# The first feed-forward product of a two-layer encoder by Strassen's algorithm in Winograd's form, over pairs of weight units

## The chip, the cores and the metric

One core of a Trainium2 chip runs the whole program. The metric is device time in microseconds (us) for one execution. The engines are TensorE (PE, matrix products; PEld is its weight load), VectorE (DVE), ScalarE (ACT), GpSimd (POOL) and SyncE (SP, here a DMA queue).

## The reference

Two post-norm layers over 512 tokens of 1024 features. Each layer has a token mixer (differential attention in layer 0, dilated window attention in layer 1), cross-attention into 256 memory tokens, and a gated feed-forward part with a centred depthwise convolution of width 3:

```python
def conv_glu(x, w_in, conv_w, conv_b, w_out):
    gate, val = jnp.split(x @ w_in, 2, axis=-1)
    gate = lax.conv_general_dilated(gate, conv_w[:, None, :], ...) + conv_b
    return (jax.nn.gelu(gate, approximate=False) * val) @ w_out
...
x = layer_norm(ALPHA * x + conv_glu(x, ...), ln_g[i, 2], ln_b[i, 2])
```

`w_in` is 1024 x 5632 (2816 gate columns and 2816 value columns) and `w_out` is 2816 x 1024. All data are float32.

## The kernel before

**Products.** Each float32 operand is split into a high part, rounded to the multiplier's format, and the low rest. `evac(src, hi, lo)` does it: ACT casts (L220), DVE subtracts (L221). `mm3` then adds three products in one PSUM bank (L241 high by high, L242 high by low, L243 low by high).

**Weights.** All weights lie in one array in the order of use. `fetch` brings the next unit of 128 x 1024 into one of four `raw` buffers through SP's queue, `split` makes its halves in one of six `whi` and `wlo` buffers, `unit()` hands out the oldest and keeps four more coming (`pump`).

**The feed-forward part.** `ffn` goes over 22 column blocks j of 128. Block j needs one unit of gate columns and one of value columns. `t_proj` multiplies a unit with all 512 tokens: 8 steps over the features, 3 products each, all 512 columns wide, into one bank. The activations `act` (`x1h`, `x1l` in layer 0) hold the 1024 features as 8 tiles of 128 by 512 tokens. `tail` then makes the hidden block: ACT scales the gate (L934), DVE adds the two neighbours (L936, twice), ACT applies gelu (L937), DVE multiplies with the value (L939), ACT and DVE split the result (L941, L942). Blocks 0 and 1 are multiplied in two halves of 256 tokens by `Halves`, the first half while the normalization before it still turns the last tokens. The hidden blocks' halves are then the stationary side of the second product (`OutNorm.finish`).

**Order.** The program on PE stands as it is written. On the other engines a scheduler sets the order from priorities; each engine then runs its list strictly in that order, and semaphores hold an instruction until its inputs are there and its output's buffer is free.

Of the kernel before, what the change touches and what calls it, by code (L numbers as in the profile page):

```python
# [20 lines left out]
NJ = FF // 128  # L21
# [128 lines left out]
def encoder(ctx: ExitStack, tc: tile.TileContext, wall, xin, lam, subln, conv, lngb, tabf, tabd, eye, out):  # L150
# [19 lines left out]
        nc.tensor.matmul(ps, warm[:, :128], warm, start=True, stop=True)  # L170


    state = {"off": 0, "n": 0}
# [43 lines left out]
    def evac(ps, hi, lo, scale=None):  # L217

        if scale is None:
            nc.scalar.copy(hi, ps)  # L220
            nc.vector.tensor_tensor(lo, ps, hi.bitcast(F32), op=ALU.subtract)  # L221
# [15 lines left out]
        while due:  # L237
            due.pop(0)[1]()

    def mm3(ps, ah, al, bh, bl, start, stop):  # L240
        nc.tensor.matmul(ps, ah, bh, start=start, stop=False)  # L241
        nc.tensor.matmul(ps, ah, bl, start=False, stop=False)  # L242
        nc.tensor.matmul(ps, al, bh, start=False, stop=stop)  # L243
        n = 1
        for d in ps.shape[1:]:
            n *= d
        tick(max(3 * 216 * n // 512, 324))

    def bank(pool, tag):
        return pool.tile([128, 512], F32, tag=tag, name="ps_" + tag)  # L250

    def sl(k, n=128):
        return slice(k * n, k * n + n)

    def t_proj(ps, act, n=SEQ):

        xh, xl = act
        wh, wl = unit()
        for k in range(8):
            mm3(ps[:, :n], wh[:, sl(k)], wl[:, sl(k)], xh[:, k, :n], xl[:, k, :n], k == 0, k == 7)  # L260
            yield 3 * 216 * n // 512

    class Halves:


        def __init__(self, pss, act):
            self.pss, self.act = pss, act
            self.us = [unit() for _ in pss]
            self.half(0)
# [8 lines left out]
    def run(gen):  # L278
        for _ in gen:
            pass  # L280
# [26 lines left out]
        for fill in fills[cur:]:  # L307
            run(fill[0])

    def new_act(name):  # L310
        h = acts.tile([128, 8, 512], F32R, tag="ah", name=name + "h")
        l = acts.tile([128, 8, 512], F32R, tag="al", name=name + "l")
        return h, l

    def places(where):

# [11 lines left out]
    class OutNorm:  # L328

        def __init__(self, ln, nk, ktile):
            self.ln, self.nk, self.ktile = ln, nk, ktile
# [104 lines left out]
        def turn(self, q, n, xs, act, ps):  # L438
            tps = ps.rearrange("p (a b) -> p a b", b=128)
            for k in range(4):  # L440
                nc.tensor.transpose(tps[:, k, :], xs[:, sl(n * 4 + k)], ident)
            pe["now"] += 440
            d = (slice(None), sl(n, 4), sl(q))
            with tc.high_priority(offset=URGENT):
                evac(tps, act[0][d], act[1][d])


    def mem_load(mt):
# [474 lines left out]
        run(late)  # L923


    def ffn(l, act, pz, hs, led):
        with ExitStack() as c:
            gp = c.enter_context(tc.tile_pool(name=f"gp{l}", bufs=2, reuse_waits="tile"))
            cw = gp.tile([128, NJ, 4], F32, name="cw", bufs=1)
            nc.scalar.dma_start(cw, conv[l])  # L930

            def tail(j, pg, pv):
                g = gp.tile([128, 512], F32, tag="g", name="g")
                nc.scalar.activation(g, pg, AF.Identity, bias=cw[:, j, 3:4], scale=cw[:, j, 1:2])  # L934
                for w, d, n in ((2, g[:, 0:511], pg[:, 1:512]), (0, g[:, 1:512], pg[:, 0:511])):
                    nc.vector.scalar_tensor_tensor(d, n, cw[:, j, w:w + 1], d, op0=ALU.mult, op1=ALU.add)  # L936
                nc.scalar.activation(g, g, AF.Gelu)  # L937
                h = gp.tile([128, 512], F32, tag="h", name="h")
                nc.vector.tensor_tensor(h, g, pv, op=ALU.mult)  # L939
                hi, lo = hs(j)  # L940
                nc.scalar.copy(hi, h)  # L941
                nc.vector.tensor_tensor(lo, h, hi.bitcast(F32), op=ALU.subtract)  # L942

            led.half(1)
            pss = led.pss
            tail(0, pss[0], pss[1])
            tail(1, pss[2], pss[3])
# [9 lines left out]

    act = new_act("x")
    res = xin
    mems = [{}, {}]  # L960
    U = [1024] * 8
    for l in range(2):
        if l == 0:
            expect(*U, *U, *([1024] * 4))
        else:
            for p in range(LH // 2):
                expect(*([1024] * (6 if p % 2 else 12)))
        expect(*U, lambda m=mems[l]: mem_load(m.get("mt")))
        expect(*U, *U, *U, *U, *([1024] * (3 * NJ)))
    for l in range(2):  # L970
        mt_kv = mems[l]
        oT = new_act(f"o{l}")
# [2 lines left out]
        with ExitStack() as cz:  # L975
# [40 lines left out]
                mem_values(mt_kv["mt"], kv, pz)  # L1016
            oT = new_act(f"c{l}")
            o2 = oT
            on = OutNorm(3 * l + 1, 8, lambda k, o_=o2: (o_[0][:, k, :], o_[1][:, k, :]))
# [3 lines left out]
            act, res, led = on.finish(lambda q: [bank(pz, "t" if q == 2 else "o") for _ in range(2)],  # L1023
                                      [(((0, 0), (1, 0)), (2, 3))], res, False,
                                      lambda q: (pa, "a") if q == 0 else (pz, "s"),
                                      lambda a: Halves([bank(pa, "a"), bank(pz, "o"), bank(pa, "a"), bank(pz, "o")], a))
            c2.close()
            with ExitStack() as c:
                fp = c.enter_context(tc.tile_pool(name=f"ff{l}", bufs=1, reuse_waits="tile"))
                f8 = new_act(f"f{l}")  # L1030
                g8 = [fp.tile([128, 2, 512], F32R, tag=f"g{n}", name="g") for n in range(NJ - 8)]

                def hs(j, f8=f8, g8=g8):
                    return tuple(x[:, j, :] for x in f8) if j < 8 else (g8[j - 8][:, 0, :], g8[j - 8][:, 1, :])

                ffn(l, act, pz, hs, led)
# [3 lines left out]
                act, res, led = OutNorm(3 * l + 2, NJ, hs).finish(  # L1040
                    lambda q: [bank(*where[q]) for _ in range(2)], first, res, l == 1,
                    lambda q: where[q] if q < 2 else (pz, "s"),
                    lambda a: Halves([bank(pa, "a"), bank(pa, "a"), bank(pz, "t"), bank(pz, "t")], a) if a else None,
                    lambda n, dt=F32: fp.tile([128, D], dt, tag=f"g{n}", name="row"))
            if l == 0:
                cpz = cz.pop_all()

# [33 lines left out]
```

## Time and profile before

| | |
|---|---|
| three runs, median | 1879.43 us (1879.33 to 1879.47) |
| the profiled execution | 1878.97 us, its span 1877.1 us |
| PE busy | 1859.6 us, 99% of the span |
| DVE, ACT, POOL busy | 51%, 40%, 6% of the span |
| granted TensorE clock | 0.999 |

A row of grouped instructions has the line, engine, operation, the tile written and the tiles read, shapes, the count, total busy us and mean ns of one; what follows the second bar is the engine's idle time ahead of them and what ended it. A row of the timeline has its start and length in us; x counts merged instructions.

### The profile page before, as it was taken

The page shows a single profiled execution, that of the slowest core. Times are in us where ns is not written, and L with a number is a line of the kernel's source. Part 1 is how long each engine was busy: PE and PEld are TensorE (multiplying, and loading weights), DVE is VectorE, ACT ScalarE, POOL GpSimd, SP SyncE. Part 2 cuts the span into 40 slices and gives each one's busy share as a digit, 9 for nine tenths or more (in the row PEclk, how much of TensorE's full clock was granted, in tenths as well). Part 3 has the DMA queues.
Part 4 walks back from the last instruction along what each step waited for, and adds up shares of the span by engine and source line. Part 5 has one row for each costly group of instructions (what it writes and reads, how often), then busy time and mean ns, then how long its engine had stood idle before and what let it go on. Part 6 is the DMA issues. An engine that isn't in the chain of part 4 may idle for free.

```text
span 1877.1 us, 25119 instructions
## 1 busy us (share of the span) xinstructions
PE 1859.6 (99%) x9896; PEld 1582.4 (84%) x9896; DVE 950.0 (51%) x1761; ACT 751.9 (40%) x1356; POOL 116.6 (6%) x192
## 2 busy tenths in 40 slices
PE   9999999999999999999999999999999999999998
PEld 7888888889888888898898898987888898888886
DVE  5687684556444432533444444444855564444324
ACT  4476554424333322324434344344544343333211
POOL 0011120010000000100000000002200100000000
PEclk9999999999999999999999999999999999999999
DMA  7233175134232334333223222232752253323241
GB/s 247 72 92 89 35 251 173 60 123 156 93 101 93 98 101 145 104 130 102 79 82 95 83 85 85 80 91 57 245 182 79 104 156 101 93 98 101 90 146 45
DMA packets 60293, 208.55 MB, mean 111 GB/s; under 512 B 8336, under 2 KB 8976, under 8 KB 60176
## 3 DMA queue, kind: packets, MB, share of 16 engines
q1 hardware_dynamic: 48512, 172.19, 29.1%
q0 software_dynamic: 10944, 33.76, 5.4%
q8 instruction: 78, 1.28, 0.3%
q10 hardware_dynamic: 720, 1.01, 0.2%
q14 instruction: 39, 0.32, 0.1%
HBM read 190.01 MB, written 12.71 MB: 108 GB/s over the span
## 4 chain that ended last, share of the span: by engine, by line
PE 90%; DVE 5%; issue 2%; ACT 1%; DMA 1%; POOL 1%; POOLq 0%; DVEq 0%; ACTq 0%
PE ps_a L241 17%; PE ps_a L242 16%; PE ps_a L243 16%; PE ps_o L241 7%; PE ps_o L243 7%; PE ps_o L242 7%; PE ps_s L243 2%; PE ps_s L242 2%; PE ps_s L241 2%; PE ps_t L243 2%; PE ps_t L241 2%; PE ps_t L242 2%; PE S L714 1%; PE ps_t L801 1%; PE ps_t L782 1%
## 5 line engine op out<-in xcount | busy, mean ns | idle before, releaser
L221 DVE TENSOR_TENSOR wlo<-raw,whi 128x1024 fp32r<-128x1024 f32 (+1 forms) x309 | 376.8, 1220 | 468.2 <-ACT whi L220 463.3
L220 ACT CAST whi<-raw 128x1024 fp32r<-128x1024 f32 (+1 forms) x309 | 323.2, 1048 | 588.7 <-PE ps_a L242 258.3
L241 PE MATMUL ps_a<-x2h,whi 128*128 128x512 f32 (+1 forms) x384 | 149.3, 389 | 0.0
L243 PE MATMUL ps_a<-x2h,wlo 128*128 128x512 f32 (+1 forms) x384 | 146.5, 381 | 0.0
L242 PE MATMUL ps_a<-x2l,whi 128*128 128x512 f32 (+1 forms) x384 | 146.3, 381 | 0.0
L241 PE MATMUL ps_a<-whi,x2h 128*128 128x512 f32 (+1 forms) x256 | 88.8, 347 | 0.0
L242 PE MATMUL ps_a<-wlo,x2h 128*128 128x512 f32 (+1 forms) x256 | 87.2, 341 | 0.0
L243 PE MATMUL ps_a<-whi,x2l 128*128 128x512 f32 (+1 forms) x256 | 87.2, 341 | 0.0
L243 PEld LDWEIGHTS ps_a<-x2h,wlo 128*128 128x128 f32 x384 | 72.2, 188 | 14.1
L241 PEld LDWEIGHTS ps_a<-x2h,whi 128*128 128x128 f32 x384 | 72.3, 188 | 13.9
L242 PEld LDWEIGHTS ps_a<-x2l,whi 128*128 128x128 f32 x384 | 72.3, 188 | 12.8
L728 ACT ACTIVATE u<-u,st 128x256 f32<-128x256 f32 x128 | 63.6, 499 | 22.8 <-DVE st L726 22.7
L241 PE MATMUL ps_o<-x1h,whi 128*128 128x512 f32 (+1 forms) x192 | 71.6, 373 | 0.0
L241 PE MATMUL ps_o<-x4h,whi 128*128 128x512 f32 (+1 forms) x192 | 71.6, 373 | 0.0
L242 PE MATMUL ps_a<-x1l,whi 128*128 128x512 f32 (+1 forms) x192 | 71.3, 371 | 0.0
L242 PE MATMUL ps_a<-x4l,whi 128*128 128x512 f32 (+1 forms) x192 | 71.3, 371 | 0.0
L241 PE MATMUL ps_a<-x1h,whi 128*128 128x512 f32 (+1 forms) x192 | 71.3, 371 | 0.0
L241 PE MATMUL ps_a<-x4h,whi 128*128 128x512 f32 (+1 forms) x192 | 71.3, 371 | 0.0
L243 PE MATMUL ps_a<-x1h,wlo 128*128 128x512 f32 (+1 forms) x192 | 71.3, 371 | 0.0
L243 PE MATMUL ps_a<-x4h,wlo 128*128 128x512 f32 (+1 forms) x192 | 71.3, 371 | 0.0
L243 PE MATMUL ps_o<-x1h,wlo 128*128 128x512 f32 (+1 forms) x192 | 71.3, 371 | 0.0
L243 PE MATMUL ps_o<-x4h,wlo 128*128 128x512 f32 (+1 forms) x192 | 71.3, 371 | 0.0
(422 smaller groups left out, 4483.7 us busy)
## 6 DMA issues: line engine op xcount, KB each, us to landing
raw<-in_wall_dram SPq DMA_DIRECT2D x314, 512.0 KB, 3.5
y<-row POOLq DMA_DIRECT2D x40, 256.0 KB, 2.8
row<-y POOLq DMA_DIRECT2D x20, 512.0 KB, 5.6
row<-in_lngb_dram POOLq DMA_DIRECT2D x12, 512.0 KB, 4.9
k<-k SPq DMA_DIRECT2D x16, 256.0 KB, 2.9
F<-fd POOLq DMA_DIRECT2D x16, 256.0 KB, 5.0
row<-in_x_dram POOLq DMA_DIRECT2D x4, 512.0 KB, 8.6
out_dram<-row SPq DMA_DIRECT2D x8, 256.0 KB, 2.0
```

The source lines that it names most:

```text
L220: nc.scalar.copy(hi, ps)
L221: nc.vector.tensor_tensor(lo, ps, hi.bitcast(F32), op=ALU.subtract)
L241: nc.tensor.matmul(ps, ah, bh, start=start, stop=False)
L242: nc.tensor.matmul(ps, ah, bl, start=False, stop=False)
L243: nc.tensor.matmul(ps, al, bh, start=False, stop=stop)
L714: nc.tensor.matmul(Ss[b, c][:, f], q_[h, b, :], k_[h], start=True, stop=True)
L728: nc.scalar.activation(u[:, f], u[:, f], AF.Exp, bias=m, scale=-1.0, accum_out=s[:, b, 2 * c + 1:2 * c + 2])
L782: nc.tensor.transpose(tp[:, k, :], u[:, sl(k)], ident)
L801: nc.tensor.matmul(o[sl(c, 64), sl(2 * (n // 2) + x)], V[:, :64], PTs[2 * x + c][:, n, :], start=n % 2 == 0, stop=n % 2 == 1)
```

## The change

Blocks 2 to 20 of each layer, 19 pairs of a gate unit and a value unit, are no longer multiplied by `t_proj`. A pair is a 2 by 2 block matrix: gate and value, each with its first four feature tiles (`a`) and its last four (`b`). The activations are 2 by 2 as well: features 0 to 511 and 512 to 1023, tokens 0 to 255 (`h0`) and 256 to 511 (`h1`). Winograd's form of Strassen's algorithm forms this product with seven half products of 4 feature tiles by 256 tokens in place of eight.

* `pair` fetches both units, forms four sums of weights on POOL (s1 to s4, L957, in the order s1, s2, s4, s3) and splits three of the four halves and the four sums, in pieces of 512 columns: seven `evac`. The sums live in two buffers. Up to two pairs are kept ahead.
* The four sums of activations (T1 to T4) are formed on POOL once per layer (L1002), from copies `xr` of the activations that ACT makes in `OutNorm.turn` (L447).
* `early`, `seventh`, `middle` and `last` are the products and the additions that join them, on ACT (L1025, L1034, L1035) and DVE (L1026, L1041, L1047). Round m multiplies early(m), seventh(m-1), middle(m), last(m-1), so that a pair's end lies in the round after its start. Each pair has two banks, and a third product may add to a bank only after the sum before it is read.
* `mix` replaces `tail`, with the gate now read from the SBUF tile `G`. The split of the hidden blocks moves to `part`, after the pairs: blocks 0 to 7 before the last block's gate product is through, 8 to 19 after its value product, 20 and 21 at the very end. Block 21 is multiplied as before.

The diff, cut:

```diff
-    def ffn(l, act, pz, hs, led):
...
-            for j in range(2, NJ):
-                pg, pv = bank(pa, "a"), bank(pz, "o")
-                run(t_proj(pg, act))
-                run(t_proj(pv, act))
-                tail(j, pg, pv)
+    def ffn(l, act, pz, H, f8, led, raw, store, pairs, ready):
...
+        def sums():
+            return [sw.tile([128, 512], F32R, tag=t, name=t, bufs=n) for t, n in (("sh", 5), ("sl", 6))]
+        def pair():
+            if len(pairs) > 1:
+                return False
+            g, v = fetch(1024), fetch(1024)
+            a, b = slice(0, 512), slice(512, 1024)
+            with tc.high_priority(offset=LATER):
+                gh, gl = halves()
+                vh, vl = halves()
+                for s in (b, a):
+                    evac(g[:, s], gh[:, s], gl[:, s])
+                S = [sums() for n in range(4)]
+                s1, s2, s4, s3 = (gp.tile([128, 512], F32, tag="s", name="s") for n in range(4))
+                for n, (o, p, q, op) in enumerate(((s1, v[:, a], v[:, b], ALU.add), (s2, s1, g[:, a], ALU.subtract),
+                                                   (s4, g[:, b], s2, ALU.subtract),
+                                                   (s3, g[:, a], v[:, a], ALU.subtract))):
+                    nc.gpsimd.tensor_tensor(o, p, q, op=op)
+                for n, o in enumerate((s1, s2, s3, s4)):
+                    evac(o, *S[n])
+                    if n == 1:
+                        evac(v[:, b], vh[:, a], vl[:, a])
...
+        def product(ps, a, b, more=False):
+            for k in range(4):
+                t = sl(k)
+                mm3(ps, a[0][:, t], a[1][:, t], b[0][:, k, :], b[1][:, k, :], k == 0 and not more, k == 3, more)
...
+        def mix(j, pg, pv):
+            g = gp.tile([128, 512], F32, tag="g", name="g", bufs=1)
+            nc.scalar.activation(g, pg, AF.Identity, bias=cw[:, j, 3:4], scale=cw[:, j, 1:2])
+            for w, d, n in ((2, g[:, 0:511], pg[:, 1:512]), (0, g[:, 1:512], pg[:, 0:511])):
+                nc.vector.scalar_tensor_tensor(d, n, cw[:, j, w:w + 1], d, op0=ALU.mult, op1=ALU.add)
+            nc.scalar.activation(g, g, AF.Gelu)
+            nc.vector.tensor_tensor(H(j), g, pv, op=ALU.mult)
+        def part(j):
...
+            nc.scalar.copy(hi, H(j))
+            nc.vector.tensor_tensor(lo, H(j), hi.bitcast(F32), op=ALU.subtract)
...
+        for o, p, q in ((T1, raw[0][:, :, h1], raw[0][:, :, h0]), (T2, raw[1][:, :, h1], T1),
+                        (T3, raw[1][:, :, h1], raw[0][:, :, h1]), (T4, raw[1][:, :, h0], T2)):
+            nc.gpsimd.tensor_tensor(o, p, q, op=ALU.subtract)
+        for n, t in enumerate((T1, T2, T3, T4)):
+            evac(t, T[0][:, n], T[1][:, n])
...
+        def early(m):
...
+            product(YZ[:, h1], A[1], B21)
+            product(XV[:, h0], A[0], B11)
+            with tc.high_priority(offset=URGENT):
+                nc.scalar.copy(G[:, h0], YZ[:, h1])
+                nc.vector.tensor_tensor(G[:, h0], G[:, h0], XV[:, h0], op=add)
+        def middle(m):
+            product(YZ[:, h0], A[3], B[0])
+            product(XV[:, h0], A[4], B[1], True)
...
+                nc.scalar.copy(y, YZ[:, h0])
+                nc.scalar.copy(G[:, h1], XV[:, h0])
+        def seventh(m):
+            product(XV[:, h0], A[5], B[2], True)
...
+                nc.vector.tensor_tensor(XV[:, h1], y, XV[:, h0], op=add)
+        def last(m):
+            product(YZ[:, h0], A[6], B22, True)
...
+                nc.vector.tensor_tensor(G[:, h1], G[:, h1], YZ[:, h0], op=add)
+            product(XV[:, h0], A[2], B[3], True)
+            mix(m + 2, G, XV)
```

**What stands where.** DVE's list in the feed-forward part of layer 0, before, over two blocks: `wlo` is a unit's low half, `g` the gate, `h` the hidden block.

```order
L936 SCALAR_TENSOR_TENSOR g_4927<-ps_a_4865,cw_4323,g_4927 128x511 x2
L939 TENSOR_TENSOR h_4932<-g_4927,ps_o_4866 128x512
L221 TENSOR_TENSOR wlo94_4971<-raw93_4968,whi94_4970 128x1024
L942 TENSOR_TENSOR g_4306<-h_4932,g_4306 128x512
L221 TENSOR_TENSOR wlo95_5012<-raw94_5009,whi95_5011 128x1024
L936 SCALAR_TENSOR_TENSOR g_4998<-ps_a_4936,cw_4323,g_4998 128x511 x2
```

DVE's list in the same part, now, over one round. `s_4891` is s4 of the pair that is being multiplied (call it pair m); `s_5028`, `s_5029`, `s_5031` are s1, s2 and s3 of pair m+1; `raw88` to `raw91` are units of the pairs behind it.

```order
L221 TENSOR_TENSOR sl_4888<-s_4891,sh_4887 128x512
L221 TENSOR_TENSOR wlo90_5153<-raw89_5148,whi90_5152 128x512
L221 TENSOR_TENSOR sl_5021<-s_5028,sh_5020 128x512
L221 TENSOR_TENSOR sl_5023<-s_5029,sh_5022 128x512
L1047 TENSOR_TENSOR G_5048<-G_5048,ps_s_5047 128x256
L221 TENSOR_TENSOR sl_5025<-s_5031,sh_5024 128x512
L978 SCALAR_TENSOR_TENSOR g_5278<-G_5048,cw_4296,g_5278 128x511 x2
L980 TENSOR_TENSOR h_5006<-g_5278,ps_s_5046 128x512
L1026 TENSOR_TENSOR G_5324<-G_5324,ps_t_5322 128x256
L221 TENSOR_TENSOR wlo92_5289<-raw90_5284,whi92_5288 128x512 x2
L1041 TENSOR_TENSOR ps_o_5184<-y_5250,ps_o_5184 128x256
L221 TENSOR_TENSOR sl_5027<-s_5030,sh_5026 128x512
```

The last row is the first row's counterpart, one round on. Between them stand the splits of a pair's weights and sums, and, among them, the additions that PE waits for (L1026, L1041).

ACT's list, before, over one block:

```order
L220 CAST whi94_4970<-raw93_4968 128x1024
L941 CAST g_4306<-h_4932 128x512
L220 CAST whi95_5011<-raw94_5009 128x1024
L934 ACTIVATE g_4998<-ps_a_4936,cw_4323 128x512
L937 ACTIVATE g_4998<-g_4998 128x512
```

ACT's list, now, over the same round as DVE's above:

```order
L220 CAST whi90_5152<-raw89_5148 128x512
L220 CAST sh_4887<-s_4891 128x512
L220 CAST sh_5020<-s_5028 128x512
L1034 COPY y_5250<-ps_o_5185 128x256
L220 CAST sh_5022<-s_5029 128x512
L1035 COPY G_5186<-ps_o_5184 128x256
L220 CAST sh_5024<-s_5031 128x512
L976 ACTIVATE g_5278<-G_5048,cw_4296 128x512
L1025 COPY G_5324<-ps_t_5323 128x256
L979 ACTIVATE g_5278<-g_5278 128x512
L220 CAST whi92_5288<-raw90_5284 128x512 x2
```

The gate's scaling and gelu (L976, L979) now stand behind the casts of s1, s2 and s3, and the copy of the next pair's first product (L1025) stands between them.

POOL's list, now (before, it has only DMAs and powers of single elements, none of them inside the feed-forward product):

```order
L957 TENSOR_TENSOR s_4891<-raw84_4869,s_4890 128x512
L957 TENSOR_TENSOR s_4892<-raw84_4869,raw85_4871 128x512
L957 TENSOR_TENSOR s_5028<-raw87_5010 128x512
L957 TENSOR_TENSOR s_5029<-s_5028,raw86_5008 128x512
L957 TENSOR_TENSOR s_5030<-raw86_5008,s_5029 128x512
L957 TENSOR_TENSOR s_5031<-raw86_5008,raw87_5010 128x512
```

The sums share two buffers, so each waits until an older one is split: by the program's waits `s_5028` waits for DVE's split of `s_4892`, `s_5029` for that of `s_4891`, `s_5030` for that of `s_5028`, `s_5031` for that of `s_5029`.

More of the change, by code (lines that the diff above doesn't have):

```diff
@@ L238, in flush, with mm3 @@
             due.pop(0)[1]()
[L240 to L243, printed above, removed]
+    def mm3(ps, ah, al, bh, bl, start, stop, more=False):
+        nc.tensor.matmul(ps, ah, bh, start=start, stop=False, skip_group_check=more)
+        nc.tensor.matmul(ps, ah, bl, start=False, stop=False, skip_group_check=more)
+        nc.tensor.matmul(ps, al, bh, start=False, stop=stop, skip_group_check=more)
         n = 1
@@ L308, in weave, with new_act @@
             run(fill[0])
[L310 to L313, printed above, removed]
+    def new_act(name, side=None):
+        state["side"] = 1 - state["side"] if side is None else side
+        return tuple(acts.tile([128, 8, 512], F32R, tag=f"a{x}{state['side']}", name=name + x, bufs=1) for x in "hl")
     def places(where):
@@ L445, in turn @@
                 evac(tps, act[0][d], act[1][d])
+                if self.keep:
+                    nc.scalar.copy(self.keep[n][:, :, sl(q)], tps)
     def mem_load(mt):
@@ L959, in encoder @@
     res = xin
-    mems = [{}, {}]
+    mems, ready = [{}, {}], [{}, {}]
     U = [1024] * 8
@@ L968, in encoder @@
         expect(*U, lambda m=mems[l]: mem_load(m.get("mt")))
-        expect(*U, *U, *U, *U, *([1024] * (3 * NJ)))
+        expect(*U, *U, *U, *U, *([1024] * 4), *([lambda r=ready[l]: "pair" in r and r["pair"]()] * (NJ - 3)),
+               *([1024] * (NJ + 2)))
     for l in range(2):
@@ L1018, in encoder @@
             o2 = oT
-            on = OutNorm(3 * l + 1, 8, lambda k, o_=o2: (o_[0][:, k, :], o_[1][:, k, :]))
+            raw = []
+            on = OutNorm(3 * l + 1, 8, lambda k, o_=o2: (o_[0][:, k, :], o_[1][:, k, :]), raw)
             with ExitStack() as c:
@@ L1022, in encoder @@
                 cross_attention(act, kv, oT, pz, ap, on)
[L1023 to L1026, printed above, removed]
             c2.close()
@@ L1029, in encoder, with store, H, rows @@
                 fp = c.enter_context(tc.tile_pool(name=f"ff{l}", bufs=1, reuse_waits="tile"))
[L1030 to L1036, printed above, removed]
+                def store(n, name, k=4):
+                    return fp.tile([128, k, 512], F32, tag=f"g{n}", name=name)
+                raw.extend(store(n, "xr") for n in (3, 4))
+                act, res, led = on.finish(
+                    lambda q: [bank(pz, "t" if q == 2 else "o") for _ in range(2)],
+                    [(((0, 0), (1, 0)), (2, 3))], res, False, lambda q: (pa, "a") if q == 0 else (pz, "s"),
+                    lambda a: Halves([bank(pa, "a"), bank(pz, "o"), bank(pa, "a"), bank(pz, "o")], a))
+                hT, f8 = {}, {}
+                def H(j, hT=hT, store=store):
+                    if j // 4 not in hT:
+                        hT[j // 4] = store(j // 4, "h", 4 if j < 20 else 2)
+                    return hT[j // 4][:, j % 4, :]
+                f, kt = ffn(l, act, pz, H, f8, led, raw, store, [], ready[l])
+                rw = {}
+                def rows(n, dt=F32, rw=rw, fp=fp, store=store):
+                    if dt != F32:
+                        return fp.tile([128, D], dt, tag="g4", name="sq")
+                    if n // 2 not in rw:
+                        rw[n // 2] = store(n // 2, "row")
+                    return rw[n // 2].rearrange("p k t -> p (k t)")[:, sl(n % 2, D)]
                 where = [(pa, "a"), (pz, "s"), (pz, "t"), (pz, "o")]
@@ L1043, in encoder @@
                     lambda a: Halves([bank(pa, "a"), bank(pa, "a"), bank(pz, "t"), bank(pz, "t")], a) if a else None,
-                    lambda n, dt=F32: fp.tile([128, D], dt, tag=f"g{n}", name="row"))
+                    rows)
+                f.close()
             if l == 0:
```

94 lines of the change are left out of this document (71 added, 23 removed).

## Prediction

> **What bounds the kernel now.** I read the page's span, its first part and the chain first.
>
> ```profile
> span 1877.1 us, 25119 instructions
> PE 1859.6 (99%) x9896; PEld 1582.4 (84%) x9896; DVE 950.0 (51%) x1761; ACT 751.9 (40%) x1356; POOL 116.6 (6%) x192
> PE 90%; DVE 5%; issue 2%; ACT 1%; DMA 1%; POOL 1%; POOLq 0%; DVEq 0%; ACTq 0%
> ```
>
> PE is busy for 99% of the span and holds 90% of the chain that ended last, so only less work on PE, or new waits on it, can move the time. The stage that changes, from the windows view (PE, PEld, DVE, ACT, POOL busy with instructions, clock, DMA):
>
> ```profile
> 500.00:550.00 50.00, 50.00 (x222) 41.42 (x221) 23.24 (x27) 17.96 (x23) 0.00 (x0) 1.00 0.31 97
> ```
>
> PE has no gap there; DVE works 23.24 us of 50, ACT 17.96, POOL not at all. How long a block takes is read from ACT's timeline, by the gate's scaling in two blocks that follow each other, and the pace of 256 columns from three products of `Halves`:
>
> ```profile
> 546.88 0.78 ACT L934 ACTIVATE g<-ps_a,cw 128x512 f32<-128x512 f32 x1
> 557.75 0.77 ACT L934 ACTIVATE g<-ps_a,cw 128x512 f32<-128x512 f32 x1
> ...
> 442.04 0.28 PE L242 MATMUL ps_a<-x1l,whi 128*128 128x256 f32 x1
> 442.16 0.28 PE L243 MATMUL ps_a<-x1h,wlo 128*128 128x256 f32 x1
> 442.28 0.28 PE L241 MATMUL ps_a<-x1h,whi 128*128 128x256 f32 x1
> ```
>
> A block is 48 products of 512 columns in 557.75 - 546.88 = 10.87 us. Products of 256 columns start 0.12 us apart, a little over half of 10.87 / 48 = 0.226.
>
> **What PE saves.** A pair becomes 7 x 4 x 3 = 84 products of 256 columns: 84 x 0.12 = 10.08 us for 10.87. That is 0.79 us a pair, 30 us over 2 x 19 = 38 pairs, and it comes only if everything else keeps a round at 10.08 us.
>
> **The other engines' load.** Durations of the operations that are added, or of their nearest kin:
>
> ```profile
> L221 DVE TENSOR_TENSOR o1l<-O,o1h 128x512 fp32r<-128x512 f32 x8 | 5.5, 692 | 4.6 <-ACT o1h L220 4.5
> L221 DVE TENSOR_TENSOR kv<-ps_a,kv 128x256 fp32r<-128x256 f32 x16 | 6.7, 419 | 0.0
> L936 DVE SCALAR_TENSOR_TENSOR g<-ps_a,cw,g 128x511 f32<-128x511 f32 x88 | 65.7, 747 | 1.5
> L939 DVE TENSOR_TENSOR h<-g,ps_o 128x512 f32<-128x512 f32 x44 | 30.2, 687 | 80.7 <-PE ps_o L243 79.3 <-ACT g L937 1.4
> L220 ACT CAST o1h<-O 128x512 fp32r<-128x512 f32 x8 | 5.0, 620 | 31.4 <-DVE O L814 31.4
> L805 ACT COPY O<-ps_t 128x256 f32<-128x256 f32 x8 | 3.0, 373 | 22.3 <-PE ps_t L801 22.3
> L934 ACT ACTIVATE g<-ps_a,cw 128x512 f32<-128x512 f32 x44 | 34.1, 775 | 0.0
> L937 ACT ACTIVATE g<-g 128x512 f32<-128x512 f32 x44 | 27.9, 634 | 86.3 <-DVE g L936 86.3
> L590 DVE TENSOR_TENSOR rr<-rr,rc 128x1 f32<-128x1 f32 x32 | 5.1, 158 | 14.0 <-POOL rr L589 13.9
> L589 POOL TENSOR_TENSOR rr<-ss,mhalf x32: 547/548/1039, 68.5 to 234.6; 128x1 f32<-128x1 f32 x32
> ```
>
> Per pair DVE does 7 splits x 0.692 + 3 additions x 0.419 + 2 x 0.747 + 0.687 = 8.28 us, ACT 7 x 0.620 + 3 x 0.373 + 0.775 + 0.634 = 6.87 us. Both fit into 10.08, so by load alone neither is the bound.
>
> A POOL sum of 512 columns is nowhere in the trace. The last row (shortest, median, longest of 32) gives 0.548 us for one element. DVE's 512 elements cost 0.692 - 0.158 = 0.534 us more than its one. At DVE's pace per element a POOL sum takes 0.548 + 0.534 = 1.08 us; with elements for nothing 0.55; at twice DVE's pace 1.62. I take 1.08, the only value with both parts from rows, and keep 0.55 and 1.62. Four sums are 4.3 us a pair.
>
> **The ring.** Load isn't the limit; order is. Follow DVE's list in the section on the change from `sl_4888` to its counterpart `sl_5027`, through what each waits for:
>
> * the split `sl_4888` (0.692) frees the buffer for POOL's s2, `s_5029` (P); ACT casts it (0.620); DVE splits it, `sl_5023` (0.692);
> * that frees the buffer for POOL's s3, `s_5031` (P); ACT casts it (0.620); behind that cast stands ACT's L976 (0.775);
> * DVE's two L978 (2 x 0.747) wait for L976; ACT's copy L1025 (0.373) waits for them, since it writes the tile `G` whose buffer they read; gelu L979 (0.634) stands behind the copy;
> * DVE's L980 (0.687) waits for gelu; behind it in DVE's list L1026 (0.419), two splits (1.384), L1041 (0.419), and `sl_5027`.
>
> The sum is 0.692 + 0.620 + 0.692 + 0.620 + 0.775 + 1.494 + 0.373 + 0.634 + 0.687 + 0.419 + 1.384 + 0.419 = 8.81 us, plus 2 P. Eight handovers from engine to engine (0.04 to 0.08 us in the timeline below) are about offset by neighbours on DVE that overlap. With P = 1.08 the ring is 10.97 us, with 0.55 it is 9.9, with 1.62 it is 12.05. No step of it can be passed over: each list is run in order. PE waits in every round for L1026, which stands in the ring, so once the two pairs kept ahead are used up PE goes at the ring's pace. Even without more, then, a round is no shorter than the block's 10.87.
>
> **The port.** Now POOL beside DVE, from the timeline of layer 0's attention and first normalization:
>
> ```profile
> 114.56 0.15 DVE L587 TENSOR_SCALAR ss<-ss 128x1 f32<-128x1 f32 x1
> 114.67 0.76 DVE L569 SCALAR_TENSOR_TENSOR u<-u,rc 128x512 f32<-128x512 f32 x1
> 114.79 1.04 POOL L589 TENSOR_TENSOR rr<-ss,mhalf 128x1 f32<-128x1 f32 x1 [4.13 <-DVE ss L587]
> 115.87 0.16 DVE L590 TENSOR_TENSOR rr<-rr,rc 128x1 f32<-128x1 f32 x1 [0.44 <-POOL rr L589]
> ...
> 131.20 0.69 DVE L221 TENSOR_TENSOR o0l<-ps_t,o0h 128x512 fp32r<-128x512 f32 x1
> 131.25 0.55 POOL L589 TENSOR_TENSOR rr<-ss,mhalf 128x1 f32<-128x1 f32 x1 [4.96 <-DVE ss L587]
> ...
> 273.68 1.21 DVE L221 TENSOR_TENSOR wlo<-raw,whi 128x1024 fp32r<-128x1024 f32 x1
> 273.85 1.47 POOL L432 TENSOR_TENSOR sm<-sm,mhalf 128x1 f32<-128x1 f32 x1 [6.63 <-DVE sm L431]
> ```
>
> The same one-element POOL operation takes 0.55 us beside a DVE operation that reads one operand from PSUM, 1.04 beside one of 0.76 us whose two operands are both in SBUF, and 1.47 beside one of 1.21: it ends 0.40 and 0.43 us after the DVE operation does. POOL is held until DVE is through. The seven splits of a pair and both L978 are of that kind (7 x 0.692 + 1.494 = 6.34 us), all of POOL's sums are its counterpart.
>
> That DVE is held by POOL the other way round, no row here shows. The Trainium skill ("SBUF — State Buffer", section "Who interferes with whom") states that a VectorE operation with two SBUF inputs and a GpSimd operation that reads SBUF exclude each other, and that whichever issues second waits for the whole of the first. By the rows alone the sum would be the one-way case below, by the page the two-way case; the rows agree with it as far as they reach.
>
> In the ring, one way: s2 starts when `sl_4888` ends, but the next split in DVE's list starts at that moment too, ahead of POOL's handover, and holds it 0.6 us. The ring is 11.6. Two ways, besides: s1 of the pair behind starts when `sl_5025` ends, which is about when L976 ends, and stands before the first L978 for nearly its whole length, 1.0 us; s4 starts when `sl_5021` ends and takes 1.08; `sl_5023`, due some 0.6 us after that end, when its cast is through, waits the other 0.5. The ring is 13.1. I take two ways: the two engines would otherwise have to share what the rows show DVE to hold alone.
>
> **Steps beside it.** Their cost and cover:
>
> * The splits of the hidden blocks (22 x 0.62 on ACT, 0.69 on DVE) leave the rounds for `part`. PE needs only blocks 0 to 3 at first, and has block 21's 10.87 us ahead of them. Nothing.
> * The copies `xr`: 8 casts of about 0.6 us, on ACT in the normalization, behind the casts that PE waits for. Nothing; the cover is ACT's idle time there.
> * The activations' sums: four on POOL of 1024 columns, 0.55 + 1.07 = 1.62 us each, behind s1 and s2 of the first pair, and four splits of 1024. They have the second half of `Halves` (96 x 0.12 = 11.5 us) and `early` (2.9 us) before PE needs T1 and T2. About 9 us of POOL and DVE work, some of it held at the port: I take 4 us a layer for this start and the end of the last pair, bounds 0 and 10.
> * The weights' bytes don't change. A unit's `raw` buffer now comes free only when POOL's s3 is done; the fetch lands 3.5 us later (the row below), and the next cast of it stands 0.62 + 0.775 + 1.494 + 0.373 + 0.634 = 3.9 us behind s3. Just covered.
> * POOL's DMAs for the last normalization stand behind the last sums; their tiles come free with `part`, before PE is through the second product. Nothing.
>
> ```profile
> raw<-in_wall_dram SPq DMA_DIRECT2D x314, 512.0 KB, 3.5
> ```
>
> **The sum.** 38 x (13.1 - 10.87) = 85 us, and 2 x 4 = 8: 93 us on the profiled execution's 1878.97 us, which stands 0.46 under the median. That is 1972 us.
>
> **Rivals.**
>
> * *One way only* (or a cheaper sum): a ring of 11.6, 38 x 0.73 + 8 = 36 us, 1915 us. For it: the only direction that rows show. Against it: one lock would have to be asymmetric.
> * *PE stays the bound*: faster. The place is the ring's two POOL sums; it decides when 2 P and what the port adds stay under 10.08 - 8.81 = 1.27 us, which needs P near 0.6 and no wait at the port. Then 38 x 0.79 = 30 us less, 8 for the ends: 1857 us. For it: 0.55 us as the low bound, which leaves 0.17 us. Against it: 1.04 and 1.47 us.
> * *Dearer sums*: P = 1.62 and two ways: 8.81 + 3.24 + 0.6 + 1.5 + 1.0 = 15.2, 38 x 4.3 + 8 = 171 us, 2050 us. For it: nothing in the trace bounds POOL's pace per element from above.
>
> **Chances.** The likeliest case 0.48 (its own range 1940 to 2010), one way 0.17, PE the bound 0.18, dearer sums 0.17. The range must leave out no more than 0.2: from 1880, above the faster case, to 2060, a little over the dearest. A measurement tells about 0.2% (4 us) from no change. Faster 0.17 and same 0.04 come from the third rival and the lower edge of the first, slower 0.79 from the rest.
>
> **What would show it.** In the new profile: L1025 to L1025 a round later 13 us apart, against 10.87 before; PE idle before L241 of a pair's third and fourth product, put down to DVE L1026 or ACT L1035; a POOL sum of about 1.1 us alone and longer beside splits; L221 of 512 columns over 0.7 us where a POOL sum runs. Wrong if rounds are 10.1 us and PE stays at 99%: then the sums are cheaper than a one-element row lets me think, or the port isn't held.

## The result, and the profile after

The changed kernel takes 1990.5 us (median of 4 runs, 1989.6 to 1990.8) for 1879.4 before: a ratio of 1.059, 95% interval 1.057 to 1.061. The profiled execution took 1990.26 us with a span of 1988.5. Of all runs here one, a fifth of sums_dve at 2476.2 us and a granted clock of 0.68, fell in the chip's slow state and is left out. From the page of the changed kernel, the span, the busy times and the chain that ended last:

```profile
span 1988.5 us, 28843 instructions
PE 1880.6 (95%) x11264; PEld 1669.1 (84%) x11264; DVE 1152.4 (58%) x2073; ACT 869.1 (44%) x1684; POOL 385.0 (19%) x352
PE 65%; DVE 16%; issue 7%; POOL 6%; ACT 4%; DMA 1%; POOLq 0%; ACTq 0%; DVEq 0%; SPq 0%
```

PE held 90% of the chain before and holds 65% now; DVE, POOL and ACT have 26%. What PE waits for, from the waits view (total us, times, longest):

```profile
PE ps_t L241 <- ACT G L1025: 46.0, 14, 11.4
PE ps_o L241 <- ACT G L1025: 25.4, 12, 3.3
PE ps_s L241 <- ACT G L1025: 21.3, 10, 3.4
```

Nearly all of it, 92.7 us, is one wait: `middle`'s first product writes a bank that ACT's copy L1025 still reads. The timeline has the copies of two pairs that follow each other:

```profile
545.13 0.37 ACT L1025 COPY G<-ps_t 128x256 f32<-128x256 f32 x1 [2.56 <-DVE g L978]
558.82 0.37 ACT L1025 COPY G<-ps_s 128x256 f32<-128x256 f32 x1 [2.56 <-DVE g L978]
```

A round is 13.69 us where a block took 10.87. The windows view of that round (PE, PEld, DVE, ACT, POOL busy with instructions, clock, DMA) has 84 products, as foreseen, but at a clock of 0.88:

```profile
545.50:559.19 13.69, 11.76 (x84) 11.56 (x84) 9.56 (x13) 6.10 (x14) 6.57 (x4) 0.88 0.24 78
```

38 such rounds would be 38 x (13.69 - 10.87) = 107 us longer than the blocks; the time grew by 111. DVE and POOL of this round, in one timeline each:

```profile
548.54 0.69 DVE L221 TENSOR_TENSOR sl<-s,sh 128x512 fp32r<-128x512 f32 x1
549.14 0.69 DVE L221 TENSOR_TENSOR wlo<-raw,whi 128x512 fp32r<-128x512 f32 x1
549.74 2.61 DVE L221 TENSOR_TENSOR sl<-s,sh 128x512 fp32r<-128x512 f32 x2
552.27 0.41 DVE L1047 TENSOR_TENSOR G<-G,ps_o 128x256 f32<-128x256 f32 x1
555.57 0.69 DVE L221 TENSOR_TENSOR sl<-s,sh 128x512 fp32r<-128x512 f32 x1 [2.88 <-ACT sh L220]
556.29 2.42 DVE L978 SCALAR_TENSOR_TENSOR g<-G,cw,g 128x511 f32<-128x511 f32 x2
```

```profile
549.36 1.62 POOL L957 TENSOR_TENSOR s<-s,raw 128x512 f32<-128x512 f32 x1 [4.88 <-issue]
551.67 1.84 POOL L957 TENSOR_TENSOR s<-raw,s 128x512 f32<-128x512 f32 x1 [0.69 <-DVE sl L221]
553.58 1.30 POOL L957 TENSOR_TENSOR s<-raw,raw 128x512 f32<-128x512 f32 x1
556.34 1.82 POOL L957 TENSOR_TENSOR s<-raw 128x512 f32<-128x512 f32 x1 [1.46 <-DVE sl L221]
```

The rows are s2, s4, s3 and the next pair's s1. Each engine holds the other. The two splits at 549.74 take 2.61 us for 2 x 0.69: the first cannot go on until s2 ends at 550.98. The two L978 take 2.42 for 1.49: s1 stands between them. In the other direction s2 and s4 take 1.62 and 1.84 us where s3, with DVE idle, takes 1.30. The Trainium skill ("SBUF — State Buffer", section "Who interferes with whom") has this rule, that two SBUF inputs on VectorE and a GpSimd read exclude each other and the second to issue waits for the whole of the first; these rows agree with it both ways.

Before, PE had no wait where the pairs now start. Now it waits 11.4 us there in each layer. In layer 0 the token sums L1002 on POOL stand ahead of it:

```profile
444.01 5.67 POOL L1002 TENSOR_TENSOR tr<-xr 128x1024 f32<-128x1024 f32 x2
449.63 3.39 POOL L1002 TENSOR_TENSOR tr<-xr,tr 128x1024 f32<-128x1024 f32 x1
452.99 2.27 POOL L957 TENSOR_TENSOR s<-raw,s 128x512 f32<-128x512 f32 x1
455.22 3.34 POOL L1002 TENSOR_TENSOR tr<-xr,tr 128x1024 f32<-128x1024 f32 x1
```

```profile
468.44 0.58 PE L241 MATMUL ps_t<-t0h,sh 128*128 128x256 f32 x1 [11.40 <-ACT G L1025]
```

L1025, which PE waits for, stands in ACT's list behind the casts of these sums.

### The profile page after: what moved, and what is told of

The parts are those of the page before. It is cut to its first block, busy times and chain, and to the rows that moved or that the text cites. A ratio compares the mean times of both kernels' runs of the same rounds, so it can differ in the third digit from the quotient of the medians.

```text
span 1988.5 us, 28843 instructions
## 1 busy us (share of the span) xinstructions
PE 1880.6 (95%) x11264; PEld 1669.1 (84%) x11264; DVE 1152.4 (58%) x2073; ACT 869.1 (44%) x1684; POOL 385.0 (19%) x352
## 4 chain that ended last, share of the span: by engine, by line
PE 65%; DVE 16%; issue 7%; POOL 6%; ACT 4%; DMA 1%; POOLq 0%; ACTq 0%; DVEq 0%; SPq 0%
PE ps_a L241 12%; PE ps_a L242 12%; PE ps_a L243 12%; DVE g L978 4%; POOL s L957 4%; DVE wlo L221 4%; DVE sl L221 4%; PE ps_o L241 3%; PE ps_o L243 3%; PE ps_o L242 3%; PE ps_t L241 2%; PE ps_t L243 2%; PE ps_t L242 2%; PE ps_s L241 2%; PE ps_s L243 2%
## 5 line engine op out<-in xcount | busy, mean ns | idle before, releaser
L221 DVE TENSOR_TENSOR sl<-s,sh 128x512 fp32r<-128x512 f32 x152 | 143.5, 946 | 107.0 <-ACT sh L220 102.4
L220 ACT CAST sh<-s 128x512 fp32r<-128x512 f32 x152 | 92.0, 619 | 167.3 <-POOL s L957 160.9
L957 POOL TENSOR_TENSOR s<-s,raw 128x512 f32<-128x512 f32 x38 | 60.1, 1581 | 168.5 <-issue 168.1
L978 DVE SCALAR_TENSOR_TENSOR g<-G,cw,g 128x511 f32<-128x511 f32 x76 | 86.3, 1136 | 6.6 <-ACT g L976 4.4
L432 POOL TENSOR_TENSOR sm<-sm,mhalf 128x1 f32<-128x1 f32 x24 | 17.5, 731 | 322.7 <-DVE sm L431 322.7
L957 POOL TENSOR_TENSOR s<-raw 128x512 f32<-128x512 f32 x38 | 67.0, 1764 | 64.7 <-DVE sl L221 58.5
L957 POOL TENSOR_TENSOR s<-raw,s 128x512 f32<-128x512 f32 x38 | 68.8, 1811 | 24.9 <-DVE sl L221 24.8
L566 ACT ACTIVATE u<-u,m 128x512 f32<-128x512 f32 x64 | 45.9, 719 | 43.5 <-DVE m L564 43.3
L241 PEld LDWEIGHTS ps_a<-whi,x2h 128*128 128x128 f32 x256 | 64.4, 251 | 0.5
L242 PEld LDWEIGHTS ps_a<-wlo,x2h 128*128 128x128 f32 x256 | 64.5, 252 | 0.2
```

Of the source, the lines that this page charges most:

```text
L241: nc.tensor.matmul(ps, ah, bh, start=start, stop=False, skip_group_check=more)
L242: nc.tensor.matmul(ps, ah, bl, start=False, stop=False, skip_group_check=more)
L432: nc.gpsimd.tensor_tensor(rs, ve, mhalf[:, 0:1], op=ALU.pow)
L566: nc.scalar.activation(u, u, AF.Exp, bias=m, scale=-1.0, accum_out=sm[:, c:c + 1])
L957: nc.gpsimd.tensor_tensor(o, p, q, op=op)
```

## The experiments

Four explanations fit the profile after. *The ring*: a chain of waits through the two `s` buffers and the lists that run in order, in which PE is not. *G*: L1025 waits for the L978 that read its tile, and PE for L1025. *The port*: turns between DVE's two-operand work and POOL's sums. *The clock*: PE's slower products after each gap. The last column is the mean round in layer 0, from the 6th to the 19th of ACT's copies to `y`, divided by 13.

| run | edit | time, us | ratio to before, 95% interval | round, us |
|---|---|---|---|---|
| (changed kernel) | | 1990.5 | 1.057 to 1.061 | 13.58 |
| no_sums | no sums of weights | 1862.7 | 0.990 to 0.993 | 10.23 |
| sums_unread | sums made, but not read | 1961.2 | 1.043 to 1.046 | 12.31 |
| dummy | PE's gap filled | 1994.0 | 1.061 to 1.064 | 13.67 |
| sums_dve | sums on DVE | 1872.0 | 0.995 to 0.998 | 10.35 |
| r | room for buffers, no more | 1973.7 | 1.049 to 1.052 | 13.06 |
| r_s4 | r, four `s` | 1965.3 | 1.045 to 1.048 | 12.68 |
| r_g3 | r, three `G` | 1969.6 | 1.047 to 1.051 | 12.96 |
| r_s4g3 | r, four `s`, three `G` | 1954.1 | 1.038 to 1.042 | 12.44 |
| r_gp | r, `G` in PSUM | 1923.1 | 1.022 to 1.025 | 11.53 |
| r_s4gp | r, four `s`, `G` in PSUM | 1878.0 | 0.9985 to 1.0004 | 10.00 |
| tok_dve | token sums on DVE | 1975.6 | 1.050 to 1.053 | 13.59 |
| best1 | r_s4gp, token sums on DVE | 1867.0 | 0.992 to 0.995 | 10.00 |

**No sums.**

```diff
-                s1, s2, s4, s3 = (gp.tile([128, 512], F32, tag="s", name="s") for n in range(4))
-                for n, (o, p, q, op) in enumerate(...):
-                    nc.gpsimd.tensor_tensor(o, p, q, op=op)
+                s1, s2, s4, s3 = v[:, a], g[:, a], g[:, b], v[:, a]
```

> GpSimd's four sums of weights per pair are left out; the splits read the raw pieces instead (the values are then not the product's). Everything else stays. Ring of waits through the sums: without them nothing in a round is longer than PE's 84 x 0.12 = 10.08 us, so 38 x (13.69 - 10.08) = 137 us less than 1990: about 1853, PE at 98% and a granted clock near 1.0. If the wait of the copy L1025 for G's buffer is the bound by itself: GpSimd plays no part in it, 1990 stays. If the sheer load of VectorE and ScalarE (8.28 and 6.87 us a round) is the bound: they keep it, 1980 to 1990.

1862.7 us, rounds of 10.23. All splits, copies and additions of DVE and ACT are still there, and both G tiles: the load and the wait for G by itself fall. The sums cost 128 us; of what is left above 1853, PE's wait at the start of the pairs, for the token sums on POOL, is 6.3 us in each layer.

**Sums that nobody reads.**

```diff
-                for n, o in enumerate((s1, s2, s3, s4)):
+                for n, o in enumerate((v[:, a], g[:, a], v[:, a], g[:, b])):
```

> GpSimd forms all four sums as before, but the splits read raw pieces in their place (the values are then not the product's): the port between VectorE and GpSimd is as busy, but no split waits for a sum, and no sum for a split. If the order of waits through the two s buffers makes most of the round: what is left is the port, 6.34 us of two-operand work on VectorE and 4 x 1.27 = 5.1 us of sums, which exclude each other: 11.4 us a round, 38 x (11.4 - 13.69) = -87, about 1903. If contention at the port by itself makes the round: 13.7 stays, 1990. If it is the buffers alone and the port costs nothing: 10.08 us, 1853.

1961.2 us, between the values. Without any wait of a split for a sum, or of a sum for a split, only 29 of the 128 us come back. What is left shows in the timelines of DVE, of POOL and of ACT:

```profile
562.94 1.23 DVE L221 TENSOR_TENSOR wlo<-raw,whi 128x512 fp32r<-128x512 f32 x1 [1.54 <-ACT whi L220]
564.10 3.44 DVE L978 SCALAR_TENSOR_TENSOR g<-G,cw,g 128x511 f32<-128x511 f32 x2
568.58 0.69 DVE L980 TENSOR_TENSOR h<-g,ps_t 128x512 f32<-128x512 f32 x1 [1.04 <-ACT g L979]
```

```profile
562.33 1.29 POOL L957 TENSOR_TENSOR s<-raw 128x512 f32<-128x512 f32 x1 [5.16 <-DMA raw<-in_wall_dram]
563.70 1.61 POOL L957 TENSOR_TENSOR s<-s,raw 128x512 f32<-128x512 f32 x1
565.40 1.59 POOL L957 TENSOR_TENSOR s<-raw,s 128x512 f32<-128x512 f32 x1
567.06 1.60 POOL L957 TENSOR_TENSOR s<-raw,raw 128x512 f32<-128x512 f32 x1
```

```profile
562.28 0.62 ACT L220 CAST whi<-raw 128x512 fp32r<-128x512 f32 x1 [1.97 <-DMA raw<-in_wall_dram]
```

Four sums run one behind the other, and each of DVE's three operations between them takes its turn after one: two L978 take 3.44 us for 1.49. My 11.4 us was the sum of what excludes each other; but the hold isn't spread over the round, it falls on the L978, on which L1025 and so PE wait. But the port is not all that is left. The edit makes the splits read the raw pieces to the end, so a `raw` buffer comes free, and the next unit lands, later: ACT's cast waits 1.97 us for it, and DVE stands idle for 1.54 us before the split that precedes these L978. no_sums reads the raw pieces as long and has rounds of 10.23, so the late unit alone doesn't make the round; how the 99 us divide between it and the port, this run doesn't show.

**PE's gap filled.**

```diff
+            pd = bank(pa, "a")[:, h0]
+            for k in range(18):
+                nc.tensor.matmul(pd, A[1][0][:, sl(k % 4)], B21[0][:, k % 4, :], start=k == 0, stop=k == 17)
             product(YZ[:, h0], A[3], B[0])
```

> 18 products of 256 columns (2.2 us at 0.12) more per round, into a PSUM bank that nobody reads, right before the product that waits for L1025: they fill PE's gap, so that its products after it keep their pace. Ring of waits: PE isn't in the ring, and with 102 x 0.12 = 12.2 us a round still fits into 13.69: 1990 within 8. If the slower products after each gap (about 1.6 us a round) are what lengthens the round: 38 x 1.5 = 57 us less, 1933. If PE is itself the bound in any other way: 38 x 2.2 = 84 us more, 2074.

1994.0 us. The window of one round, to be held against the one above:

```profile
545.50:559.20 13.70, 12.57 (x102) 12.25 (x102) 9.59 (x13) 6.08 (x13) 6.61 (x4) 1.00 0.23 78
```

The clock is 1.00, PE does 102 products in place of 84, and the round is 13.70. PE is not what sets it; the slow products are an effect.

**Sums on VectorE.**

```diff
-                    nc.gpsimd.tensor_tensor(o, p, q, op=op)
+                    nc.vector.tensor_tensor(o, p, q, op=op)
```

> The four sums on VectorE in place of GpSimd, two s buffers, two G tiles: no GpSimd at the port in the rounds. VectorE's load becomes 8.28 + 4 x 0.69 = 11.05 us a round. If GpSimd's pace and its turns at the port make most of the loss: a round is 11.05 to 12, 1890 to 1926, faster than now although VectorE does more. If the order of waits through s and G makes it whatever engine adds: 13 and more, 1965 to 1990.

1872.0 us, below the 1890 that I gave as the lower end, and 0.4% faster than before the change. The buffers and the tiles G are those of the changed kernel. With POOL's pace and its turns, though, the handovers are gone as well: a sum and the split whose buffer it takes now stand in one engine's list. Two groups and a window:

```profile
L957 DVE TENSOR_TENSOR s<-raw,raw 128x512 f32<-128x512 f32 x38 | 26.2, 689 | 0.8
L978 DVE SCALAR_TENSOR_TENSOR g<-G,cw,g 128x511 f32<-128x511 f32 x76 | 56.7, 746 | 2.7 <-ACT g L976 2.6
```

```profile
540.00:580.00 40.00, 38.01 (x317) 37.20 (x316) 38.28 (x67) 23.32 (x46) 0.00 (x0) 1.00 0.33 106
```

The L978 are at 0.746 us, never held. DVE is busy for 38.28 of 40 us and PE for 38.01. My 11.05 us of load was too high because I added durations: DVE's operations of 0.68 us start 0.60 us apart when one follows the other.

**Buffers.** All runs with an r put s1's halves in the upper halves of the value unit's `whi` and `wlo`, which the pairs leave empty, and have fewer buffers for the sums' halves (4 and 5 as below; 4 and 4 in r_s4g3, 5 and 5 with G in PSUM). Run r does no more than that.

```diff
-                S = [sums() for n in range(4)]
+                S = [(vh[:, b], vl[:, b])] + [sums() for n in range(3)]
...
-            return [... for t, n in (("sh", 5), ("sl", 6))]
+            return [... for t, n in (("sh", 4), ("sl", 5))]
```

> Only the edit that makes room in the runs with more buffers: s1's halves go to the unused upper halves of the value unit's tiles, two s buffers and two G tiles as in the changed kernel. If the room alone changes nothing: 1990 within 5, and what those runs won (about 25 and 21 us) is due to their buffers. If the other place of s1's split in VectorE's list (now between L978 and L980) opens the ring by itself: 1965 to 1975, and the buffers won little.

> The whole computation, with four s buffers for two: a sum waits for the split of the same sum one round before, no longer for a split of its own round. Room for it is won by putting s1's halves in the unused upper halves of the value unit's tiles. Ring of waits: it opens, and a round is 11.4 to 12.0 us (port, and order in the lists): 1903 to 1926. If contention at the port makes the round: 13.2 to 13.7, 1970 to 1990. If the copy L1025's wait for G makes it: 13.7, 1990.

> The whole computation, with two s buffers as before, but three G tiles for two: the copy L1025 no longer waits for the two L978 of the pair before, which read the tile it writes (s1's halves in the unused upper halves of the value unit's tiles make room). Ring of waits through the two s buffers: only L1025's own 0.37 us leaves the ring, 13.3 us a round, 1975. If the copy's wait for G is what makes PE wait and so the round: PE's gaps close, 10.1 to 11 us, 1855 to 1890. Both needed: 13.3 here and the rest in the run with both changes.

> Four s buffers and three G tiles. With four s buffers alone a round was about 13.0 us: the sums ran back to back, each of VectorE's two-operand instructions between them took turns with a sum (0.69 to 1.74 us), and two L978 in that stretch held L1025, for which PE waits. If that chain (sum, L978, L1025, PE) is what is left: PE waits no more, and a round is 10.1 to 11.4 us (the port's 11.4 as the upper end): 1855 to 1903. If VectorE's own list is the bound while it takes turns: 12.5 to 13, 1945 to 1965.

r itself takes 17 us off, 1973.7; what it moves is s1's split, which now stands between L978 and L980 in DVE's list. s4, which waits for that split, then follows s2 at once: in r s3 starts 2.07 us after the end of s2, in the changed kernel 2.60, and this is the 0.5 us by which the mean rounds differ.

Against r, four `s` buffers win 8 us, three G tiles 4 (its interval overlaps r's), both 20. That does not make the waits through `s` small, for four buffers do not take them away, though I had expected it. By the program's waits s2 and s3 do wait for their own splits of one round before, but s1 gets the buffer in which s4 of two pairs before lay, and s4's split stands behind L980, L1026 and L1041. From the timelines of DVE, POOL and ACT in r_s4:

```profile
570.96 0.68 DVE L221 TENSOR_TENSOR sl<-s,sh 128x512 fp32r<-128x512 f32 x1
571.72 1.29 POOL L957 TENSOR_TENSOR s<-raw 128x512 f32<-128x512 f32 x1 [4.89 <-DVE sl L221]
573.04 0.62 ACT L220 CAST whi<-s 128x512 fp32r<-128x512 f32 x1 [1.53 <-POOL s L957]
573.69 0.69 DVE L221 TENSOR_TENSOR wlo<-s,whi 128x512 fp32r<-128x512 f32 x1 [2.05 <-ACT whi L220]
```

The first row is s4's split, then come s1, its cast and its split, and behind that split in DVE's list stand both L978, L980 and the next s4's split: a ring again. In r_s4g3 it returns after 12.70 us; DVE is idle in it for 2.05 us before s1's split and 0.16 before L980, and three of its operations, one L978 among them, are held for about 3.2 us together. Without these holds the ring would be some 9.5 us (an estimate), under PE's 10. With both changes, PE waits for L1026, which stands behind L980 and so behind the held L978, in place of L1025. The largest of these waits in r_s4g3, and its group of the L978:

```profile
PE ps_t L241 <- DVE G L1026: 21.2, 9, 2.5
```

```profile
L978 DVE SCALAR_TENSOR_TENSOR g<-G,cw,g 128x511 f32<-128x511 f32 x76 | 91.2, 1200 | 1.1
```

**G in PSUM.** Two banks stand idle in these rounds. L1025 and L1035 now write small tiles, and DVE's additions write G into a bank.

```diff
-            G = gp.tile([128, 512], F32, tag="G", name="G")
+            G = bank(pa, "a")
...
-                nc.scalar.copy(G[:, h0], YZ[:, h1])
-                nc.vector.tensor_tensor(G[:, h0], G[:, h0], XV[:, h0], op=add)
+                nc.scalar.copy(e, YZ[:, h1])
+                nc.vector.tensor_tensor(G[:, h0], e, XV[:, h0], op=add)
```

> G in two idle PSUM banks, as in the run of 1878 us, but with the two s buffers of the changed kernel. Ring of waits through the s buffers: it is still closed, only L1025's 0.37 us and the 1.0 us for which the first L978 was held by a sum are gone: 12.3 us a round, about 1938. If the turns at the port and the wait for G are all there is: 10.0 to 10.5 us, 1878 to 1897, with or without the two more buffers.

> Four s buffers, and G in two PSUM banks that stand idle in these rounds (the copies L1025 and L1035 go to small tiles, VectorE's additions write G). L1025 waits for no L978, and L978 reads one operand from PSUM, so by the rows it takes no turns with the sums: what excludes the sums falls from 6.34 to 7 x 0.69 = 4.84 us a round, with 5.1 of sums 9.9. If turns at the port are what is left: 10.1 to 10.6 us a round, 1855 to 1873, and below the run with three G tiles. If reading G from PSUM changes nothing there: the same as that run.

1923.1 us, below the 1938 of a ring that stays closed, and 1878.0. Against r, G in PSUM alone wins 51 us, and four `s` buffers on top another 45, where they won 8 without it. The L978 of r_s4gp in groups, one beside a sum of POOL in the timelines, and a window of its rounds:

```profile
L978 DVE SCALAR_TENSOR_TENSOR g<-ps_a,cw,g 128x511 f32<-128x511 f32 x88 | 65.4, 744 | 5.7 <-ACT g L976 4.6
```

```profile
566.67 0.75 DVE L978 SCALAR_TENSOR_TENSOR g<-ps_a,cw,g 128x511 f32<-128x511 f32 x1
```

```profile
566.04 1.76 POOL L957 TENSOR_TENSOR s<-raw,raw 128x512 f32<-128x512 f32 x1
```

```profile
540.00:580.00 40.00, 40.00 (x338) 40.00 (x338) 34.20 (x54) 25.15 (x49) 27.07 (x16) 1.00 0.33 107
```

The first L978 lies wholly within s3 and is not held: with one operand in PSUM it takes no turn. r_s4gp and r_s4g3 differ by 76 us; besides G's place and the small tiles, r_s4gp has one buffer more for each half of the sums. The wait of s1 for the older s4 is still in r_s4gp's program, but it is over in time: s1 follows s3 at once. GpSimd's pace is no bound: four sums of 1.6 to 1.8 us fit into a round of 10.00, and PE has no gap.

**Token sums.**

```diff
-            nc.gpsimd.tensor_tensor(o, p, q, op=ALU.subtract)
+            nc.vector.tensor_tensor(o, p, q, op=ALU.subtract)
```

> The changed kernel with one edit: the tokens' four sums on VectorE in place of GpSimd. PE's wait for them was 11.4 us in each layer. If it adds to the time of its layer: 2 x 10 = 20 us less, 1970. If the ring of waits behind it gives the time, so that a pair that starts sooner only waits later: the rounds before PE runs out of the pairs kept ahead are longer instead, and 0 to 8 us are won, 1982 to 1990.

> Four s buffers and G in PSUM, as in the run of 1878 us, and the tokens' four sums on VectorE in place of GpSimd. In that run the rounds were at PE's own 10.0 us, but PE waited 14.3 us in each layer for the first copy, which stood behind token sums of 2.3 to 3.4 us on GpSimd. If those sums are what is late: VectorE makes them in 4 x 1.2 = 4.9 us, within the 14 us that PE still has work for, the wait falls to 2 us or less, and the time to about 1878 - 2 x 12 = 1854. If the splits behind them, taking turns with GpSimd's sums of weights, are late as well: a wait of 8 us, 1866. If the wait is filled again by something later in the part: 1878.

In the changed kernel this wins 15 us, between the two values; PE's wait in layer 0 falls from 11.4 to 5.1 us (with 2.7 more a little later), and the rounds stay. In r_s4gp it wins 11: 14.3 us of wait in each layer become 3.5 and 3.1, probably since the splits behind the sums and ACT's list are late in turn, which no run here shows. best1 is the fastest of these kernels, and 0.65% faster than the kernel before (interval 0.5 to 0.8%).

## Why the prediction came close, and where it was off

1972 us was forecast, 1990.5 measured. Two groups first, for POOL's pace: s3 in the changed kernel, and the two token sums that read no other in r_s4gp (shortest, median, longest), neither held by DVE:

```profile
L957 POOL TENSOR_TENSOR s<-raw,raw 128x512 f32<-128x512 f32 x38 | 49.1, 1291 | 8.2 <-DVE sl L221 5.7
```

```profile
L1002 POOL TENSOR_TENSOR tr<-xr x4: 2406/2410/2412, 447.1 to 1525.5; 128x1024 f32<-128x1024 f32 x4
```

* **PE's pace** was right: in best1 a round is 10.00 us (10.08 forecast) where PE alone sets it. The 30 us are there to be had, and the changed kernel has none of them.
* **The sum on POOL** was mis-sized: 1.08 us taken, 1.29 measured alone, 0.2 us short and twice in the ring. The 1024 columns of a token sum take 2.41 us alone against 1.62. The step that failed was to take the one-element row, a power, as the fixed cost of an addition, and DVE's pace per column. From 512 to 1024 columns POOL takes (2.41 - 1.29) / 512 = 2.2 ns a column, twice DVE's 1.04. The Trainium skill ("GPSIMD Engine Reference", section "Elementwise — side-by-side cycle accounting") gives 4497 ns for 2048 columns; a quarter and a half of it, 1.12 and 2.25 us as estimates, would have been nearer than my row.
* **The ring** was 13.1 us forecast, 13.69 measured. s2 held by a split (0.3 us where 0.6 was priced) and the L978 held by s1 (0.9 for 1.0) came as written. Two links were wrong. s4 stands between s2 and s3 in POOL's list, and s3 waits for it, not for the split's buffer. And `sl_5023` isn't held by s4 but holds it: the split ahead of it had been held by s2, so that both came late.
* **What holds the round** is the ring, as forecast, and "PE goes at the ring's pace" held: the rows from one split of s4 to the next form a chain without PE. DVE's three additions of PE's products, L1026, L1041 and L1047, kept DVE waiting for PE in no round of layer 0 once the pairs kept ahead were used up, and in run dummy PE did 18 products more in the same round. The ring is also what r_s4 and r_s4g3 are left with. There L1047 waits for PE in 3 and 2 of 19 rounds, so that a second loop through L1047, L976, L978, L1025 and PE is close, but seldom the one that decides.
* **PE's wait** was named wrongly: L1025, not L1026 or L1035. The wait for L1025 covers the whole bank, so `middle`'s first product stands for it before the fourth can stand for L1026.
* **The ends** were 4 us a layer; PE's wait is 11.4, above my bound of 10. By tok_dve 15 us of the time hang on it.
* **Steps at no cost** held: no wait of PE for the deferred splits, the copies `xr` or POOL's row DMAs is in the waits view.
* **Rivals.** One way only: refuted by two L978 in 2.42 us, and in 3.44 where the sums run back to back. Dearer sums: not reached. PE the bound: its condition, a sum of about 0.6 us and no wait at the port, is what sums_dve made, and its price was 1857 us for 1872 measured; r_s4gp met it in another way, by taking the L978 from the port.

The arithmetic came within 18 us for partly wrong reasons: 38 x 0.6 = 22 us too little for the rounds and about 15 for the ends; against them stand the first round in each layer, 8.3 us for 13.7 while the pairs kept ahead last, 11 us that I had not counted, and some shorter rounds besides.

Left open: how much of r_gp's 51 us is the small tile for L1035, or its one more buffer for the sums' high halves, which weren't run alone; and how the loss divides between the turns at the port and the waits of the ring in which they stand. No run has either of them alone; with no sums on POOL, or with G in PSUM and four `s` buffers, the loss is gone.

## What to carry to other kernels

Work moved to GpSimd isn't free because GpSimd is idle: where it reads SBUF, each VectorE operation with two SBUF operands beside it takes a turn, and what counts is who waits for that operation. Look for the held operation on the path that the bottleneck engine waits for, and move one of its operands to PSUM, or give the extra work to VectorE itself, whose load of 96% cost less here than a second engine at its port. A test that makes the work but lets nobody read it parts contention from order only if it leaves every buffer free as early as before, and more buffers open a ring only if the program's waits show it: read there which buffer each tile gets.

## What the runs showed of the hardware that I had not expected

A gap of 2 us in PE's work makes its products slower some 0.6 us after the restart. From the timeline of the changed kernel:

```profile
543.36 0.28 PE L243 MATMUL ps_o<-t0h,sl 128*128 128x256 f32 x1
545.56 0.38 PE L241 MATMUL ps_t<-t0h,sh 128*128 128x256 f32 x1 [1.93 <-ACT G L1025]
...
546.27 0.41 PE L243 MATMUL ps_t<-t0h,sl 128*128 128x256 f32 x1
546.48 0.41 PE L241 MATMUL ps_t<-t0h,sh 128*128 128x256 f32 x1
...
549.66 0.28 PE L241 MATMUL ps_t<-t0h,sh 128*128 128x256 f32 x1
549.78 0.28 PE L242 MATMUL ps_t<-t0l,sh 128*128 128x256 f32 x1
```

The products start 0.21 us apart for 3.4 us, at a granted clock of 0.50, then 0.12 again. In run dummy, which fills the gap, the clock of the round is 1.00. The Trainium skill ("TensorE: Matmul & The Clock Gate", section "HAM oscillation — how this bites in real kernels") puts the limit for gaps at about 3.4 us; here 1.93 us did it, every round, and the fast pace before each gap had lasted 7.5 us. It cost nothing only because PE was not the bound.
